# A decoder trunk's MLP: squared token factors at the additions to the residual, half of the first products in 512 columns, and a new order of one block

## The chip, the core and the metric

The kernel runs on one core of a Trainium2 chip. A core has five engines that run their own instruction streams and wait for each other by semaphores: TensorE (PE, matmuls into PSUM; its weight loads are shown as PEld), VectorE (DVE), ScalarE (ACT), GpSimd (POOL) and SyncE (SP, here a queue of DMA issues). The metric is the device time of one execution in microseconds, the median of several runs; lower is better.

## The reference, cut to what matters

Two layers over x, 256 tokens by 2048 columns, in float32: a recurrent block and an attention block, each followed by an MLP, and a last RMS norm. The MLP is what the change touches:

```python
def _rmsnorm(x, g):
    y = x32 * lax.rsqrt(jnp.mean(x32 * x32, axis=-1, keepdims=True) + EPS)
    return y * g

def _mlp(h, w1, w2):                       # w1 2048 x 8192, w2 8192 x 2048
    u = jnp.einsum('bsd,df->bsf', h, w1)
    u = jnp.square(jax.nn.relu(u))
    return jnp.einsum('bsf,fd->bsd', u, w2)

x = x + _mlp(_rmsnorm(x, mlp_norm[i]), mlp_w1[i], mlp_w2[i])
```

The norm's factor of a token, rstd (the reciprocal root of its mean square), is positive. So relu(rstd * v)^2 is rstd^2 * relu(v)^2, and the factor can stand before the square or, squared, behind the second product.

## The kernel before

**Units and items.** A unit is a matrix of 128 x 2048 weights: 1 MB that SP's queue loads (`raw`, or a tile `q..`), that ScalarE copies to a rounded part (`whi`, line 134) and VectorE subtracts to a remainder (`wlo`, line 138). Each product x * w is made of three matmul passes with these parts, x high * w high, x low * w high and x high * w low. Items are the steps of the program, mostly one unit each, in an order written out by hand. Around the item of unit i the code issues the load of unit i+5, ScalarE's `whi` up to i+3 and VectorE's `wlo` up to i+2. There are three buffers each for `whi` and `wlo`, so the `whi` of unit i+3 waits until PE has done unit i. `after(n, ...)` puts work behind the item that comes n later; additions to x (`take`, `closed`) come first there. Every engine works through its instructions in program order.

**The MLP** runs in eight parts p of 1024 hidden columns. The first product of a part is eight "w" items (j = 0 to 7): 128 hidden rows each, with the weights standing and the tokens moving. `stand_w` makes for each of 16 slices of the inner dimension three matmuls of 256 columns: `whi` with the tokens' high parts, `whi` with their low parts, `wlo` with the high parts. `stand_both`, used before in the recurrent block's gates and in the attention, moves high and low parts in one matmul of 512 columns, and one of 256 for `wlo`; the two halves of the bank are summed later. `u_done` takes relu times the token's rstd from PSUM to `uu` (line 603, VectorE, with rstd spread over all partitions as `rstdB`), squares it and copies it to its high part `aT` (lines 604 and 606, ScalarE), and one item later VectorE makes the low part (line 612).

**The second product** of parts 0 to 6 uses a scheme with seven products in place of eight for two halves of the tokens, of the hidden rows and of the output columns ("groups" 0 and 1: output columns 0 to 1023 and 1024 to 2047). Its items are b11, b21, t1, t2, b22, t3 and t4, 12 matmuls of 512 columns each. Sums of weights are made by VectorE (line 693: `qT`, for b11 and b22) or by POOL's adding transfers (line 689: q12 += q22 for b22, q21 += qT for t4); sums of tokens by VectorE (lines 623 to 636: `sw`, `sT`). Results are added to x by `take` (line 697). PSUM has eight banks: four (`acc`) hold the sums B, T and C of group 0 and B of group 1 over all parts, and are added to x only at the end of part 6, `ENDS` items after their product; the others are added to x after each part. A block is the 22 items of a part:

```python
2: (
    "w", "b11 0", "t1 0", "w", "b21 0", "b22 0", "t2 0", "w", "t3 0", "w", "t4 0", "b11 1", "t1 1", "w",
    "b22 1", "t2 1", "w", "t3 1", "b21 1", "w", "w", "t4 1",
),
```

Its w's make the first products of the next part. Counted from 0, they stand at 0, 3, 7, 9, 13, 16, 19 and 20, with j = 0, 4, 1, 5, 2, 6, 3, 7. Below, w13 is the w at place 13, and so on. (In the change below, the sixth w stands at place 17; w17 is that one, w16 the one before.) In part 0 the places 2 and 3 are exchanged. The last part, 7, has plain products only.

Of the kernel before, what the change touches and what calls it, by code (L numbers as in the profile page):

```python
# [32 lines left out]
for _name, _n in (("mix0", 16), ("mix1", 16), ("mlp0", 16), ("mlp1", 16), ("lam", 20),  # L33
# [9 lines left out]
SCRATCH = 4096  # L43
LOOK_LOAD = 5

CONV = (0, 2)

BOTH = range(3, 9)

ROWS = 5  # L50

# [8 lines left out]

ORDER = {
    0: ("s", "w") * 8,
    2: (
        "w", "b11 0", "t1 0", "w", "b21 0", "b22 0", "t2 0", "w", "t3 0", "w", "t4 0", "b11 1", "t1 1", "w",
        "b22 1", "t2 1", "w", "t3 1", "b21 1", "w", "w", "t4 1",
    ),
}

SUMS = {"b22": [("q12", "q12", "q22", "dma"), ("qT", "qT", "q22", "dve")],
        "t4": [("q21", "q21", "qT", "dma")],  # L70
        "b11": [("qT", "b11", "q12", "dve")]}

HELD = {0: ("B", "T", "C"), 2: ("B",)}

ENDS = {"t1 0": 12, "b21 0": 12, "b22 0": 18, "b21 1": 3}


@with_exitstack
def trunk(ctx: ExitStack, tc: tile.TileContext, a: dict, out: bass.AP):
# [194 lines left out]
    def new_ssq():  # L274
        state["ssq"] = perm.tile([P, NT, NCH], F32, name="ssq", bufs=2)

    def rstd_cols():
        v = perm.tile([P, 4, NT], F32, name="rs", bufs=2)
        nc.vector.tensor_reduce(v[:, 0, :], state["ssq"], axis=AX.X, op=OP.add)
        nc.vector.tensor_scalar(v[:, 0, :], v[:, 0, :], 1.0 / D, EPS, op0=OP.mult, op1=OP.add)  # L280
        nc.scalar.activation(v[:, 1, :], v[:, 0, :], AF.Sqrt)
        nc.vector.reciprocal(v[:, 2, :], v[:, 1, :])
        nc.vector.tensor_mul(v[:, 3, :], v[:, 2, :], v[:, 2, :])
        nc.vector.tensor_mul(v[:, 3, :], v[:, 3, :], v[:, 0, :])
        nc.vector.tensor_scalar(v[:, 3, :], v[:, 3, :], -0.5, 1.5, op0=OP.mult, op1=OP.add)
        nc.vector.tensor_mul(v[:, 2, :], v[:, 2, :], v[:, 3, :])
        state["rstd"] = v[:, 2, :]

    def rstd_rows():
        state["kick"] = True  # L290
# [22 lines left out]
            mm(ps, hi[:, s], xl, False, False)  # L313
            mm(ps, lo[:, s], xh, False, last and j == len(ks) - 1)

    def stand_both(ps, u):

        hi, lo = split[u]
        state["kick"] = False
        for k in range(KD):  # L320
            x, s = xT(k), slice(k * 128, (k + 1) * 128)
            mm(ps, hi[:, s], x.rearrange("p (t u q) -> p u q t", t=2, u=2), k == 0, False)
            mm(ps[:, :S], lo[:, s], moving(x, 0), False, k == KD - 1)
# [43 lines left out]
        for t in range(NT):  # L367
            nc.vector.tensor_add(xc[n][:, t, :], xc[n][:, t, :], acc[t])

    def close_chunk(n, gname, rows):  # L370
        def closed(acc):
            if n == 0:
                new_ssq()
            add_x(n, acc)
            if n < NCH - 1:
                square_sum(n)
            after(1, transpose_chunk, n, gname)
            if n == NCH - 1:
                after(1, square_sum, n)
                after(1, rstd_cols)  # L380
                if rows:
                    after(4, rstd_rows)
        return closed
# [148 lines left out]
    def plan_rec():  # L532
        def proj(h, j, g):
            u = unit(a["w_in"][(KR if g else 0) + 2 * h + j] if len(units) >= FIRST else a["w_first"][len(units)])

            done = gb_done if g else xb_done
            if u < FIRST:
                first[u] = (done, h, j)
                return

            bank = []

            def begin():
# [24 lines left out]

        def oproj(n, kq):
            u = unit(a["w_out"][n * 5 + kq])  # L570
            out_item(("o", n), u, aT, range(4 * kq, 4 * kq + 4), kq == 0, kq == 4,
                     close_chunk(n, "mlp0", True))

        for h in range(NB):
            proj(h, 0, 0)
            proj(h, 1, 0)
            proj(h, 0, 1)
            proj(h, 1, 1)
            if h:
# [18 lines left out]
    def u_done(p, j, ps):  # L598
        h, k = divmod(j, 4)
        if h == 0:  # L600
            squares[p, k] = lru.tile([P, 2, S], F32, name="uu", bufs=4)
        uu = squares[p, k][:, h, :]
        nc.vector.scalar_tensor_tensor(uu, ps[:, :S], 0.0, state["rstdB"], op0=OP.max, op1=OP.mult)
        nc.scalar.activation(uu, uu, AF.Square)
        t = new_aT(8 * (p % 2) + j)
        nc.scalar.activation(t[:, 0:256], uu, AF.Copy)
        after(1, u_low, t, uu)
        if h == 1 and GROUPS[p]:
            after(1, waiting.append, (p, k))

    def u_low(t, uu):
        nc.vector.tensor_sub(t[:, 256:512], uu, t[:, 0:256].bitcast(F32))
# [36 lines left out]
    def plan_mlp(w1, w2, done):  # L649
        def plan_first(p, j):  # L650
            u = unit(w1[8 * p + j])

            def run():
                accs["u", p, j] = acc_tile() if p == 0 else psum.tile([P, 512], F32, name="g", bufs=2)
                stand_w(accs["u", p, j][:, :S], u, range(KD), 0, True, True)
                after(0, u_done, p, j, accs.pop(("u", p, j)))
            item(u, run, "w")

        def plan_start():
            us = [unit(w1[j]) for j in (0, 4)]  # L660
            for at, ks in enumerate((range(0, 12), range(12, 16))):
                for u, j in zip(us, (0, 4)):
                    def run(u=u, j=j, ks=ks, at=at):
                        if at == 0:
                            accs["u", 0, j] = acc_tile()
                        stand_w(accs["u", 0, j][:, :S], u, ks, ks[0], at == 0, at == 1)
                        if at == 1:
                            after(1 if j == 0 else 0, u_done, 0, j, accs.pop(("u", 0, j)))
                    item(u, run)

        def plan_plain(p, n, h, last_part):
            u = unit(w2[((p // 2) * 4 + n) * 4 + (p % 2) * 2 + h])
            out_item(("m", n), u, aT, range(8 * (p % 2) + 4 * h, 8 * (p % 2) + 4 * h + 4), h == 0, h == 1,
                     done(n) if last_part else (lambda acc, n=n: add_x(n, acc)))

        def plan_group(p, n0, last_group):

# [15 lines left out]
                nc.vector.tensor_add(q[to], q[a], q[b])  # L693

            def take(n, t, b, sign):
                x = xc[n0 + n][:, t, :]
                (nc.vector.tensor_add if sign > 0 else nc.vector.tensor_sub)(x, x, bank[b])
# [200 lines left out]
    def plan_att():  # L898
# [61 lines left out]
    def final_add(acc, cols, t, base, to):  # L960

        x = xc[LAST][:, t, cols]
        nc.vector.tensor_add(x, x, acc[:, cols])
        junk = perm.tile([P, 512], mybir.dt.bfloat16, name="junk")
        nc.vector.tensor_tensor_reduce(junk[:, cols], x, x, 0.25 / D, base, OP.mult, OP.add, to)

# [284 lines left out]
```

## Time and profile before

| | |
|---|---|
| median of 3 runs | 2011.72 us (2011.59 to 2011.74) |
| the profiled execution | 2011.96 us, of which the span of its profile 2010.2 us |
| TensorE busy | 2000.4 us, 13569 matmuls, granted clock 0.999 |
| VectorE busy | 1732.4 us |
| ScalarE busy | 1291.9 us |
| HBM read | 409.59 MB, 205 GB/s over the span |
| first MLP, parts 0 to 6 | about 367 to 956 us of the span; a block repeats after 79.5 us |
| second MLP | about 1372 to 2002 us |

Busy time of TensorE is a cover, not a rate: the matmuls are pipelined, and the profile models their ends. A better measure is how long a piece of the chain takes for its number of matmuls. A row of the timeline has start, length, engine, line, operation and tiles; in brackets the idle time before it and what ended it. A row of windows has the window, its length, and per engine the busy time with the number of instructions.

### The profile page before, as it was taken

The numbers are of one execution on the slowest core, as the hardware profiler recorded it, in microseconds if no ns is written. First come the engines' busy times: TensorE is split into PE (matmuls) and PEld (weight loads), VectorE is DVE, ScalarE is ACT, GpSimd is POOL, SyncE is SP. The second block draws the span as 40 slices with busy tenths as digits, with TensorE's granted clock in tenths as the row PEclk, the third lists the DMA queues.
The fourth block names the chain that finished last, engine by engine and source line by source line (L and its number), as shares of the span: only waits on it lengthen the run. The fifth ranks groups of instructions, "written<-read, shape, count | busy, mean of one in ns | idle before, by whom it ended". The sixth has DMA issues, their size and how long they took to land.

```text
span 2010.2 us, 32554 instructions
## 1 busy us (share of the span) xinstructions
PE 2000.4 (100%) x13569; PEld 1870.2 (93%) x13569; DVE 1732.4 (86%) x1917; ACT 1291.9 (64%) x1426; POOL 95.4 (5%) x83
## 2 busy tenths in 40 slices
PE   9999999999999999999999999999999999999998
PEld 9999988999999999999889999889999999999997
DVE  7999975799999999998658969857999999999986
ACT  7788875566666666666557657656666666666663
POOL 0111110000000000000000000000000000000001
PEclk9999999999999999999999999999999999999999
DMA  8555565678788788787555555456787887887874
GB/s 311 210 189 204 190 229 197 241 248 252 264 284 268 226 293 271 247 250 244 206 213 173 187 190 183 173 199 242 250 252 262 288 266 227 295 272 246 249 245 165
DMA packets 69059, 472.51 MB, mean 235 GB/s; under 512 B 7600, under 2 KB 7984, under 8 KB 13616
## 3 DMA queue, kind: packets, MB, share of 16 engines
q1 hardware_dynamic: 60560, 411.19, 54.7%
q0 software_dynamic: 8064, 58.72, 14.9%
q8 instruction: 106, 1.74, 0.3%
q10 hardware_dynamic: 288, 0.52, 0.1%
q14 instruction: 41, 0.34, 0.0%
HBM read 409.59 MB, written 2.10 MB: 205 GB/s over the span
## 4 chain that ended last, share of the span: by engine, by line
PE 96%; DVE 3%; ACT 0%; issue 0%; DMA 0%
PE acc L203 46%; PE g L203 32%; PE tr L203 18%; DVE wlo L138 1%; PE tr L244 1%; DVE c L439 0%; PE tr L866 0%; ACT whi L134 0%; DMA xT<-in_begin 0%; DVE c L435 0%; DVE sT L636 0%; DVE glo L138 0%; DVE qT L693 0%; DVE gw L470 0%; ACT xc L979 0%
## 5 line engine op out<-in xcount | busy, mean ns | idle before, releaser
L134 ACT ACTIVATE whi<-raw 128x2048 fp32r<-128x2048 f32 (+1 forms) x309 | 568.4, 1844 | 294.7 <-PE acc L203 163.2
L138 DVE TENSOR_TENSOR wlo<-raw,whi 128x2048 fp32r<-128x2048 f32 (+1 forms) x309 | 678.1, 2198 | 92.3 <-ACT whi L134 91.9
L203 PE MATMUL g<-xT,whi 128*128 128x256 f32 x3649 | 617.0, 275 | 0.0
L203 PEld LDWEIGHTS g<-xT,whi 128*128 128x128 f32 x3649 | 554.0, 192 | 0.0
L203 PE MATMUL g<-xT,wlo 128*128 128x256 f32 x1824 | 502.9, 276 | 0.2 <-DVE wlo L138 0.2
L203 PE MATMUL acc<-xT,whi 128*128 128x256 f32 (+1 forms) x2020 | 453.7, 313 | 0.1
L203 PE MATMUL acc<-xT,wlo 128*128 128x256 f32 x1360 | 373.1, 274 | 0.5 <-DVE wlo L138 0.4
L203 PEld LDWEIGHTS g<-xT,wlo 128*128 128x128 f32 x1824 | 350.1, 192 | 1.5 <-DVE wlo L138 0.3
L203 PEld LDWEIGHTS acc<-xT,whi 128*128 128x128 f32 x2020 | 333.2, 191 | 19.1 <-ACT whi L134 1.0
L203 PE MATMUL acc<-whi,aT 128*128 128x512 f32 (+1 forms) x1086 | 322.9, 374 | 0.0
L138 DVE TENSOR_TENSOR wlo<-q,whi 128x2048 fp32r<-128x2048 f32 x112 | 256.0, 2286 | 28.0 <-ACT whi L134 27.8
L134 ACT ACTIVATE whi<-q 128x2048 fp32r<-128x2048 f32 x112 | 214.3, 1914 | 79.1 <-PE g L203 52.2
L203 PEld LDWEIGHTS acc<-xT,wlo 128*128 128x128 f32 x1360 | 261.2, 192 | 1.2 <-DVE wlo L138 1.1
L203 PEld LDWEIGHTS acc<-whi,aT 128*128 128x128 f32 x1086 | 204.0, 189 | 27.6
L203 PE MATMUL tr<-whi,sT 128*128 128x512 f32 (+1 forms) x728 | 212.7, 364 | 0.0
L203 PE MATMUL acc<-wlo,aT 128*128 128x512 f32 (+1 forms) x536 | 200.9, 376 | 0.0
L134 ACT ACTIVATE whi<-qT 128x2048 fp32r<-128x2048 f32 x56 | 107.5, 1919 | 127.7 <-PE g L203 93.2
L203 PEld LDWEIGHTS tr<-whi,sT 128*128 128x128 f32 x728 | 137.6, 189 | 20.5
L203 PE MATMUL tr<-whi,aT 128*128 128x512 f32 (+1 forms) x462 | 140.3, 373 | 0.0
L138 DVE TENSOR_TENSOR wlo<-qT,whi 128x2048 fp32r<-128x2048 f32 x56 | 128.0, 2286 | 1.3 <-ACT whi L134 1.3
L203 PE MATMUL tr<-wlo,sT 128*128 128x512 f32 x336 | 127.3, 379 | 0.0
L203 PEld LDWEIGHTS acc<-wlo,aT 128*128 128x128 f32 x536 | 101.1, 189 | 13.4 <-DVE wlo L138 0.2
(173 smaller groups left out, 2166.6 us busy)
## 6 DMA issues: line engine op xcount, KB each, us to landing
raw<-in_w SPq DMA_DIRECT2D x172, 1024.0 KB, 7.0
q<-in_w SPq DMA_DIRECT2D x84, 1024.0 KB, 8.2
raw<-in_w_in SPq DMA_DIRECT2D x35, 1024.0 KB, 4.7
raw<-in_w_qk SPq DMA_DIRECT2D x32, 1024.0 KB, 4.8
q<-q POOLq DMA_DIRECT2D x28, 1024.0 KB, 12.4
q<-qT POOLq DMA_DIRECT2D x28, 1024.0 KB, 7.5
raw<-in_w_out SPq DMA_DIRECT2D x20, 1024.0 KB, 4.7
raw<-in_w_v SPq DMA_DIRECT2D x16, 1024.0 KB, 4.8
```

Of the source, the lines that this page charges most:

```text
L134: nc.scalar.activation(split[i][0][:, s], r, AF.Copy)
L138: nc.vector.tensor_sub(split[i][1][:, s], r, split[i][0][:, s].bitcast(F32))
L203: nc.tensor.matmul(o, l, r, start=start, stop=stop, skip_group_check=True)
L244: nc.tensor.transpose(tr[:, k, t * 128:(t + 1) * 128], xc[n][:, t, c:c + 128], ident)
```

## The change

There are four edits.

1. `u_done` no longer multiplies by rstd. The additions of the MLP's products to x (`take`, `add_mlp`, `final_add`) become one instruction with a factor per token, x = product * rstd^2 + x (or with the negative of it, where the sign is minus). The factors are two more columns of `rstd_cols`; `rstd_rows`, which spread rstd over the partitions with two transposes and a copy, is not called for the MLPs.
2. The w's with j = 1, 2, 3, 6 in part 0, and with j = 1, 2, 4, 7 in the others, use `stand_both`. Their two halves are brought together by ScalarE (a copy of the second half to `uu`) and VectorE (a custom instruction, TENSOR_ADD_SAT: sum of both, held between 0 and the largest float, which is the relu). The other w's have their relu on ScalarE, straight from PSUM. For the wide ones the square follows one item later.
3. In group 1, b21 stands ahead of b22 and no longer behind t3.
4. The held banks are added to x 18 (T), 15 (B of group 0), 17 (C) and 4 items (B of group 1) after their product; before 12, 12, 18 and 3.

```diff
 ORDER = {
     0: ("s", "w") * 8,
-    2: (
-        "w", "b11 0", "t1 0", "w", "b21 0", "b22 0", "t2 0", "w", "t3 0", "w", "t4 0", "b11 1", "t1 1", "w",
-        "b22 1", "t2 1", "w", "t3 1", "b21 1", "w", "w", "t4 1",
-    ),
+    2: ("w", "b11 0", "t1 0", "w", "b21 0", "b22 0", "t2 0", "w", "t3 0", "w", "t4 0", "b11 1", "t1 1", "w", "b21 1", "b22 1", "t2 1", "w", "t3 1", "w", "w", "t4 1",),
 }
...
+WIDE = ((1, 2, 3, 6), (1, 2, 4, 7))
...
-ENDS = {"t1 0": 12, "b21 0": 12, "b22 0": 18, "b21 1": 3}
+ENDS = {'t1 0': 18, 'b21 0': 15, 'b22 0': 17, 'b21 1': 4}
...
+        if squared:
+            nc.vector.tensor_mul(v[:, 4, :], v[:, 2, :], v[:, 2, :])
+            nc.vector.tensor_scalar(v[:, 5, :], v[:, 4, :], -1.0, None, op0=OP.mult)
+            state["rstd2"] = v[:, 4:6, :]
...
+    def add_scaled(x, acc, t, sign=1):
+
+        i = 0 if sign > 0 else 1
+        nc.vector.scalar_tensor_tensor(x, acc, state["rstd2"][:, i, t:t + 1], x, op0=OP.mult, op1=OP.add)
+
+    def add_mlp(n, acc):
+        for t in range(NT):
+            add_scaled(xc[n][:, t, :], acc[t], t)
...
-                after(1, rstd_cols)
+                after(1, rstd_cols, not rows)
                 if rows:
                     after(4, rstd_rows)
...
-        nc.vector.scalar_tensor_tensor(uu, ps[:, :S], 0.0, state["rstdB"], op0=OP.max, op1=OP.mult)
+        if j in WIDE[p > 0]:
+            nc.scalar.activation(uu, ps[:, S:], AF.Copy)
+            after(0, u_sum, p, j, ps, uu)
+        else:
+            after(0, u_plain, p, j, ps, uu)
+
+    def u_plain(p, j, ps, uu):
+        nc.scalar.activation(uu, ps[:, :S], AF.Relu)
+        u_square(p, j, uu)
+
+    def u_sum(p, j, ps, uu):
+        nc.vector._custom_dve(TENSOR_ADD_SAT, out=uu, in0=ps[:, :S], in1=uu, s0=LARGEST, s1=0.0)
+        after(1, u_square, p, j, uu)
+
+    def u_square(p, j, uu):
+        h, k = divmod(j, 4)
         nc.scalar.activation(uu, uu, AF.Square)
         t = new_aT(8 * (p % 2) + j)
         nc.scalar.activation(t[:, 0:256], uu, AF.Copy)
         after(1, u_low, t, uu)
...
-                stand_w(accs["u", p, j][:, :S], u, range(KD), 0, True, True)
-                after(0, u_done, p, j, accs.pop(("u", p, j)))
+                first_product(accs["u", p, j], u, j, p)
+                u_done(p, j, accs.pop(("u", p, j)))
...
+        def first_product(ps, u, j, p, ks=range(KD)):
+            if j in WIDE[p > 0]:
+                stand_both(ps, u, ks)
+            else:
+                stand_w(ps[:, :S], u, ks, ks[0], ks[0] == 0, ks[-1] == KD - 1)
...
             def take(n, t, b, sign):
-                x = xc[n0 + n][:, t, :]
-                (nc.vector.tensor_add if sign > 0 else nc.vector.tensor_sub)(x, x, bank[b])
+                add_scaled(xc[n0 + n][:, t, :], bank[b], t, sign)
```

How the order changes shows at two places. The first is behind w13 of a block. On TensorE (`g` is the w's bank, `tr` and `acc` those of products) there stands before, where w13 ends and b22 1 begins:

```order
L203 MATMUL g<-xT_3869,whi 128x256 x2
L203 MATMUL g<-xT_3869,wlo 128x256
L203 MATMUL tr<-whi,sT_4038 128x512
L203 MATMUL tr<-wlo,sT_4038 128x512
L203 MATMUL tr<-whi,sT_4038 128x512
```

and in the change, where w13 is a wide one and b21 1 (the tokens' `aT`, in a held bank) begins:

```order
L204 MATMUL g<-xT_3869,whi 128x512
L204 MATMUL g<-xT_3869,wlo 128x256
L204 MATMUL acc<-whi,aT_4444 128x512
L204 MATMUL acc<-wlo,aT_4444 128x512
L204 MATMUL acc<-whi,aT_4444 128x512
```

Two matmuls of 256 columns have become one of 512, and b22 1 comes one product later. On VectorE there stands before at this place, from the `wlo` of w13 to that of w16 (the additions are line 697):

```order
L138 TENSOR_TENSOR wlo<-raw,whi 128x2048
L693 TENSOR_TENSOR qT<-qT,q_5506 128x2048
L697 TENSOR_TENSOR xc_70<-xc_70,tr 128x512
L138 TENSOR_TENSOR wlo<-q_5506,whi 128x2048
L697 TENSOR_TENSOR xc_71<-xc_71,tr 128x512
L138 TENSOR_TENSOR wlo<-qT,whi 128x2048
L603 SCALAR_TENSOR_TENSOR uu<-g,rstdB 128x256
L138 TENSOR_TENSOR wlo<-raw,whi 128x2048
```

and in the change, from the `wlo` of w13 to that of t2 1 (`q_5294` is b21 1's weights, `q_5372` b22 1's; line 630 is the custom sum, 378 the addition with a factor):

```order
L139 TENSOR_TENSOR wlo<-raw,whi 128x2048
L378 SCALAR_TENSOR_TENSOR xc_70<-tr,rs,xc_70 128x512
L139 TENSOR_TENSOR wlo<-q_5294,whi 128x2048
L733 TENSOR_TENSOR qT<-qT,q_5372 128x2048
L378 SCALAR_TENSOR_TENSOR xc_71<-tr,rs,xc_71 128x512
L139 TENSOR_TENSOR wlo<-q_5372,whi 128x2048
L630 ISA uu<-g,uu 128x256
L139 TENSOR_TENSOR wlo<-qT,whi 128x2048
```

The `wlo` of b21 1 has come in ahead of the sum of weights, and the addition of t1 1's bank (the second of the two; b22 1 writes to that bank next) now has w13 and b21 1 between its product and b22 1, before w13 alone. The second place is the end of the block, on VectorE. Before, from the `wlo` of the next block's first w (its j = 0) to the token sum behind the `wlo` of its b11:

```order
L138 TENSOR_TENSOR wlo<-raw,whi 128x2048
L693 TENSOR_TENSOR qT<-raw,q_5784 128x2048
L612 TENSOR_TENSOR aT_5842<-uu,aT_5842 128x256
L603 SCALAR_TENSOR_TENSOR uu<-g,rstdB 128x256
L138 TENSOR_TENSOR wlo<-raw,whi 128x2048
L697 TENSOR_TENSOR xc_70<-xc_70,tr 128x512
L612 TENSOR_TENSOR aT_5905<-uu,aT_5905 128x256
L623 TENSOR_TENSOR sw<-uu 128x2x128
```

and in the change:

```order
L139 TENSOR_TENSOR wlo<-raw,whi 128x2048
L733 TENSOR_TENSOR qT<-raw,q_5608 128x2048
L646 TENSOR_TENSOR aT_5666<-uu,aT_5666 128x256
L630 ISA uu<-g,uu 128x256
L670 TENSOR_TENSOR sT_5673<-sw,sT_5673 128x512
L139 TENSOR_TENSOR wlo<-raw,whi 128x2048
L378 SCALAR_TENSOR_TENSOR xc_70<-tr,rs,xc_70 128x512
L657 TENSOR_TENSOR sw<-uu 128x2x128
```

Here w20 has the custom sum in place of line 603, the low part of the third token sum stands one item later, and the low part of w20's `aT` has left this piece (it stands behind the next block's first w).

More of the change, by code (lines that the diff above doesn't have):

```diff
@@ L9 @@
 from concourse._compat import with_exitstack
+from concourse.dve_ops import TENSOR_ADD_SAT
 F32 = mybir.dt.float32
@@ L25 @@
 EPS = 1e-6
+LARGEST = float(np.finfo(np.float32).max)
 KD = D // 128
@@ L44 @@
 LOOK_LOAD = 5
+BOTH = range(3, 9)
 CONV = (0, 2)
-BOTH = range(3, 9)
 ROWS = 5
@@ L62 @@
     0: ("s", "w") * 8,
-    2: (
-        "w", "b11 0", "t1 0", "w", "b21 0", "b22 0", "t2 0", "w", "t3 0", "w", "t4 0", "b11 1", "t1 1", "w",
-        "b22 1", "t2 1", "w", "t3 1", "b21 1", "w", "w", "t4 1",
-    ),
+    2: ("w", "b11 0", "t1 0", "w", "b21 0", "b22 0", "t2 0", "w", "t3 0", "w", "t4 0", "b11 1", "t1 1", "w", "b21 1", "b22 1", "t2 1", "w", "t3 1", "w", "w", "t4 1",),
 }
-SUMS = {"b22": [("q12", "q12", "q22", "dma"), ("qT", "qT", "q22", "dve")],
+SUMS = {"b22": [("q12", "q12", "q22", "dma"), ("qT", "qT", "q22", ('dve', 'dve'))],
         "t4": [("q21", "q21", "qT", "dma")],
         "b11": [("qT", "b11", "q12", "dve")]}
+WIDE = ((1, 2, 3, 6), (1, 2, 4, 7))
 HELD = {0: ("B", "T", "C"), 2: ("B",)}
-ENDS = {"t1 0": 12, "b21 0": 12, "b22 0": 18, "b21 1": 3}
+ENDS = {'t1 0': 18, 'b21 0': 15, 'b22 0': 17, 'b21 1': 4}
 @with_exitstack
@@ L275, in new_ssq, with rstd_cols @@
         state["ssq"] = perm.tile([P, NT, NCH], F32, name="ssq", bufs=2)
-    def rstd_cols():
-        v = perm.tile([P, 4, NT], F32, name="rs", bufs=2)
+    def rstd_cols(squared=False):
+        v = perm.tile([P, 6, NT], F32, name="rs", bufs=2)
         nc.vector.tensor_reduce(v[:, 0, :], state["ssq"], axis=AX.X, op=OP.add)
@@ L314, in stand_w, with stand_both @@
             mm(ps, lo[:, s], xh, False, last and j == len(ks) - 1)
-    def stand_both(ps, u):
+    def stand_both(ps, u, ks=range(KD)):
         hi, lo = split[u]
         state["kick"] = False
-        for k in range(KD):
+        for k in ks:
             x, s = xT(k), slice(k * 128, (k + 1) * 128)
@@ L368, in add_x, with close_chunk @@
             nc.vector.tensor_add(xc[n][:, t, :], xc[n][:, t, :], acc[t])
-    def close_chunk(n, gname, rows):
+    def add_scaled(x, acc, t, sign=1):
[4 more added lines that the diff above has]
+            add_scaled(xc[n][:, t, :], acc[t], t)
+    def close_chunk(n, gname, add):
+        rows = add is add_mlp
         def closed(acc):
@@ L373, in closed @@
                 new_ssq()
-            add_x(n, acc)
+            add(n, acc)
             if n < NCH - 1:
@@ L571, in oproj @@
             out_item(("o", n), u, aT, range(4 * kq, 4 * kq + 4), kq == 0, kq == 4,
-                     close_chunk(n, "mlp0", True))
+                     close_chunk(n, "mlp0", add_x))
         for h in range(NB):
@@ L608, in u_done @@
         if h == 1 and GROUPS[p]:
-            after(1, waiting.append, (p, k))
+            if j in WIDE[p > 0]:
+                waiting.append((p, k))
+            else:
+                after(1, waiting.append, (p, k))
     def u_low(t, uu):
@@ L654, in run @@
                 accs["u", p, j] = acc_tile() if p == 0 else psum.tile([P, 512], F32, name="g", bufs=2)
-                stand_w(accs["u", p, j][:, :S], u, range(KD), 0, True, True)
-                after(0, u_done, p, j, accs.pop(("u", p, j)))
+                first_product(accs["u", p, j], u, j, p)
+                u_done(p, j, accs.pop(("u", p, j)))
             item(u, run, "w")
+        def first_product(ps, u, j, p, ks=range(KD)):
+            if j in WIDE[p > 0]:
+                stand_both(ps, u, ks)
+            else:
+                stand_w(ps[:, :S], u, ks, ks[0], ks[0] == 0, ks[-1] == KD - 1)
         def plan_start():
@@ L665, in run @@
                             accs["u", 0, j] = acc_tile()
-                        stand_w(accs["u", 0, j][:, :S], u, ks, ks[0], at == 0, at == 1)
+                        first_product(accs["u", 0, j], u, j, 0, ks)
                         if at == 1:
-                            after(1 if j == 0 else 0, u_done, 0, j, accs.pop(("u", 0, j)))
+                            u_done(0, j, accs.pop(("u", 0, j)))
                     item(u, run)
@@ L673, in plan_plain @@
             out_item(("m", n), u, aT, range(8 * (p % 2) + 4 * h, 8 * (p % 2) + 4 * h + 4), h == 0, h == 1,
-                     done(n) if last_part else (lambda acc, n=n: add_x(n, acc)))
+                     done(n) if last_part else (lambda acc, n=n: add_mlp(n, acc)))
         def plan_group(p, n0, last_group):
@@ L704, in make_all @@
                 def make_all():
-                    for m in SUMS.get(name, []):
-                        add(*m)
+                    for *m, by in SUMS.get(name, []):
+                        add(*m, by if isinstance(by, str) else by[n0 // 2])
                 u = form(load_all, make_all, lambda: q[source])
@@ L925, in oproj @@
             u = unit(a["w_o"][n * 4 + kq])
-            out_item(("a", n), u, aT, range(4 * kq, 4 * kq + 4), kq == 0, kq == 3, close_chunk(n, "mlp1", True))
+            out_item(("a", n), u, aT, range(4 * kq, 4 * kq + 4), kq == 0, kq == 3, close_chunk(n, "mlp1", add_x))
         for n in (0, 1):
@@ L941, in done @@
                 new_ssq()
-            add_x(n, acc)
+            add_mlp(n, acc)
             square_sum(n)
@@ L962, in final_add @@
         x = xc[LAST][:, t, cols]
-        nc.vector.tensor_add(x, x, acc[:, cols])
+        add_scaled(x, acc[:, cols], t)
         junk = perm.tile([P, 512], mybir.dt.bfloat16, name="junk")
@@ L1046, in trunk @@
     item(None, lambda: lru.open("mlp"))
-    plan_mlp(a["w1_0"], a["w2_0"], lambda n: close_chunk(n, "mix1", True))
+    plan_mlp(a["w1_0"], a["w2_0"], lambda n: close_chunk(n, "mix1", add_mlp))
     item(None, lru.close)
```

## The prediction

> **What bounds the kernel now.** I read the page first (busy times and the chain's shares), then TensorE's own waits, then the chain in order of time, and last the queue of VectorE (DVE) at the two places where the chain's pieces are longer than their matmuls need.
>
> ```profile
> PE 2000.4 (100%) x13569; PEld 1870.2 (93%) x13569; DVE 1732.4 (86%) x1917; ACT 1291.9 (64%) x1426; POOL 95.4 (5%) x83
> PE 96%; DVE 3%; ACT 0%; issue 0%; DMA 0%
> ```
> ```profile
> PE g L203 <- DVE junk L1067: 1.3, 1, 1.3
> PE acc L203 <- DVE wlo L138: 0.4, 1, 0.4
> PE g L203 <- DVE wlo L138: 0.2, 1, 0.2
> ```
> TensorE (PE) is busy for 2000.4 of 2010.2 us and its named waits sum to 1.9 us. So time comes only from PE's own stream: fewer or cheaper matmuls, or the short delays that the modelled ends cover. Those show in the chain (start, length, engine and number of matmuls):
>
> ```profile
> 449.11 5.34 PE tr L203 x25
> ...
> 488.85 5.54 PE g L203 x48
> 494.40 5.18 PE acc L203 x24
> 502.17 5.36 PE g L203 x48
> ...
> 515.49 7.78 PE tr L203 x37
> 523.27 5.36 PE g L203 x48
> 528.63 5.33 PE tr L203 x25
> 533.96 5.36 PE g L203 x48
> 544.51 10.72 PE g L203 x96
> 557.83 5.36 PE g L203 x48
> 568.38 5.54 PE g L203 x48
> ...
> 1069.05 10.48 PE acc L203 x64
> ...
> 1891.76 5.54 PE g L203 x48
> ...
> 1931.53 5.33 PE tr L203 x25
> ```
> One first-product unit ("w") is 48 matmuls of 256 columns in 5.36 us: 111.7 ns each. The attention's q and k units do the same columns as 16 matmuls of 512 and 16 of 256: two units take 10.48, so 5.24 each. Three products of 12 matmuls take 7.78, 2.59 each; but the pair b22 1 and t2 1 behind w takes 5.33 to 5.34, 0.15 too long, in each of the 14 blocks with products (first and last shown). And the second w of a block takes 5.54, 0.18 too long, in 12 blocks.
>
> **The change part by part.** *512 columns.* Four of eight w's in each of 16 part-steps, 64 units, lose 16 matmuls each: 64 x (5.36 - 5.24) = **7.7 us** gained, all on PE. Nearest rows bound it: nothing (the columns are the same) and 7.7; I take 7.7, since the attention's units come from the same helper with operands laid out alike; a loss is excluded while a 512-column matmul takes 215.8 ns (494.40) and two of 256 take 223.4. The Trainium skill ("TensorE: Matmul & The Clock Gate", Back-to-back issue gap) puts a matmul at N/2.4 + 2.5 ns. By that two of 256 cost 2.5 ns more than one of 512, which is 2.6 us for the 1024 pairs. The trace agrees for 512 columns (494.40: 5.18 us for 24, 215.8 ns each) but has 111.7, not 109.2, for 256, and its whole units decide.
>
> *b21 1 ahead of b22 1.* What the pair waits for is on DVE:
>
> ```profile
> 525.51 2.29 DVE L138 TENSOR_TENSOR wlo<-q,whi 128x2048 fp32r<-128x2048 f32 x1
> 527.71 0.68 DVE L697 TENSOR_TENSOR xc<-xc,tr 128x512 f32<-128x512 f32 x1
> ```
> b22 1 adds to the bank that t1 1 has filled; the addition of that bank to x ends at 528.39 and PE is there at 528.63 less the lead of a weight load. With b21 1 (a held bank, nothing to wait for) in between, PE comes 2.6 us later: 14 x 0.15 = **2.1 us** gained; bounds 0 and 2.1. What is late next there: three products follow w, so DVE must give three wlo's in 7.8 us. DVE's instructions follow each other 0.08 us before the one ahead ends (558.92 + 2.28 = 561.20 against 561.12, rows below): wlo and a sum of weights take 2.20 of its queue, uu or the low part of aT 0.34, an addition 0.60, in the new form 0.67. DVE has idle time behind w7 (PE's end 507.53), so I walk from there. ScalarE's Copy and whi (0.39 + 1.92) let the wlo of t4 0 start at 509.85. To the end of b22 1's wlo stand six wlo's, two sums, four additions and two low parts: 13.2 + 4.4 + 2.7 + 0.7 = 21.0, that is 530.9. PE comes to b22 1 after t3 0, w9, three products, w13 and b21 1: 507.53 + 2.59 + 5.36 + 7.78 + 5.24 + 2.59 = 531.1, and wants wlo one matmul (0.2) later: 0.4 us to spare. For t2 1 DVE adds a custom sum and a wlo (2.6), PE a product (2.59): again 0.4. Covered, thinly; each 0.1 us beyond that costs 1.4 us over the 14 blocks.
>
> *The second w of a block.* DVE is in one unbroken run up to it:
>
> ```profile
> 541.19 2.29 DVE L138 TENSOR_TENSOR wlo<-raw,whi 128x2048 fp32r<-128x2048 f32 x1 [1.41 <-ACT whi L134]
> ...
> 552.91 0.42 DVE L603 SCALAR_TENSOR_TENSOR uu<-g,rstdB 128x256 f32<-128x256 f32 x1
> ...
> 558.25 0.42 DVE L612 TENSOR_TENSOR aT<-uu,aT 128x256 fp32r<-128x256 f32 x1
> 558.58 0.42 DVE L603 SCALAR_TENSOR_TENSOR uu<-g,rstdB 128x256 f32<-128x256 f32 x1
> 558.92 2.28 DVE L138 TENSOR_TENSOR wlo<-raw,whi 128x2048 fp32r<-128x2048 f32 x1
> 561.12 0.68 DVE L697 TENSOR_TENSOR xc<-xc,tr 128x512 f32<-128x512 f32 x1
> ...
> 565.24 0.42 DVE L603 SCALAR_TENSOR_TENSOR uu<-g,rstdB 128x256 f32<-128x256 f32 x1
> 566.18 2.28 DVE L138 TENSOR_TENSOR wlo<-raw,whi 128x2048 fp32r<-128x2048 f32 x1
> ```
> ```profile
> 541.19:568.46 27.27, 26.99 (x33) 1.00 0.97 321
> ```
> The run starts 1.87 us after PE's end of the w ahead (533.96 + 5.36 = 539.32: ACT's whi) and ends at 568.46, 29.14 after it; PE is at the second w 29.06 after it (568.38). In the change the run starts with the wlo of w20, one item later (its whi waits for the end of w17, as now that of w19 for w16). It holds one wlo less (558.92 to 561.12: 2.20), two uu less (0.34 each: w19 and w22 keep 256 columns and take ScalarE's Relu), and two additions to x that cost more:
>
> ```profile
> L697 DVE TENSOR_TENSOR xc<-xc,tr x140: 678/680/683, 408.4 to 1962.8; 128x512 f32<-128x512 f32 x140
> L788 DVE SCALAR_TENSOR_TENSOR av<-acc,rs,av x8: 741/746/751, 1039.7 to 1185.8; 128x512 fp32r<-128x512 f32 x8
> L965 DVE CUSTOM_DVE_ANT_0 junk<-xc,fs x3: 485/485/752, 1997.7 to 2002.8; 128x256 bf16<-128x256 f32 x2, 128x512 bf16<-128x512 f32 x1
> ```
> An addition with a factor per token is of L788's form: 0.07 more. The sum of the halves (w20) is a custom instruction: between uu's 0.42 and L965's 0.49. So the run is 27.27 - 2.20 - 0.68 + 0.14 = 24.53, or 24.60. PE's way loses b21 1 (2.59) and 0.12 for w20: 29.06 - 2.71 = 26.35. The run ends 1.87 + 24.53 = 26.40 to 26.47 after the start: 0.05 to 0.12 behind PE, against 0.08 now. So this wait stays: 0.15 to 0.22 for 0.18. I put down **0.3 us** lost in 12 blocks (0.02 each); bounds: gone (2.2 gained) and 0.1 worse (1.2 lost).
>
> *Factors at the additions.* rstd's rows are no longer spread for the two MLPs: 4 transposes leave PE.
>
> ```profile
> 366.48 0.22 PE tr L293 x2
> ```
> 2 x 0.22 = **0.4 us** gained. Two small instructions more in the column of factors lie ahead of the first addition by a whole block. The 128 uu leave DVE, 64 custom sums come; ScalarE gets 64 Relu and 64 Copy of 0.39 us:
>
> ```profile
> L792 ACT ACTIVATE y<-acc 128x256 f32<-128x256 f32 x32 | 12.3, 386 | 0.7
> ```
> That is 8 x 0.39 = 3.1 us in a block of 79.5 (568.38 less 488.85), on an engine at 64%. It is not on the path where ScalarE's whi ends DVE's idle time (541.19): the w ahead of it keeps 256 columns, so no Copy stands before that whi. If that cover went, 0.39 x 12 = 4.7 us. The last addition of the kernel, behind the last matmul, costs 0.06 more: **0.1 lost**. The held banks' new places (18, 15, 17 and 4 items after their product) only move ten additions (five per MLP) within the last block with products, in which DVE makes no token sums: nothing; if all stood in PE's way, 10 x 0.75 = 7.5 us, or as much gained if they stand in it now.
>
> **Sum**: 7.7 + 2.1 + 0.4 - 0.3 - 0.1 = 9.8 us. The profiled execution took 2011.96 (span 2010.2): 2002.2, span 2000.4. The runs' median is 0.24 lower: **2001.9**.
>
> **The rivals.** *The second w's wait goes* (DVE gains more than I count): 2.2 and the 0.3 more, **1999.4**. For it: DVE loses 64 instructions. Against: the run starts with ScalarE's whi, not with DVE's backlog, so earlier savings don't enter it.
>
> *512 columns give less.* If only a third of the 7.6 ns per pair came from the split, and the rest from the alternation of whi and wlo weights, which stays, 5.1 of the 7.7 us would be missing: **2007.0**. Against it: the units at 1069.05 alternate just so and take 5.24. The rule of the Trainium skill's page named above would leave just such a third.
>
> *DVE or ScalarE late at the second w.* The Square of w20 now stands one item later, behind the whi of t1, and the token sums on DVE wait for it; that whi waits for DVE's sum for b11, so the Square is done some 2.4 us (1.92 and itself) behind it, while DVE has a low part, the custom sum, a low part of 512 columns, wlo and an addition to make first (0.34 + 0.34 + 0.60 + 2.20 + 0.67 = 4.1): 1.7 us to spare. If other waits ate that and 0.6 us more: 12 x 0.6 = 7.2 lost, **2009.1**, no change.
>
> *A transfer takes the place of the wait: slower.* b21 1's load now stands on SP's queue ahead of t2 1's, and waits for the buffer that t4 0 frees:
>
> ```profile
> 504.94 0.42 SPq L685 DMA_DIRECT2D q<-in_w  x1
> ...
> 511.73 0.33 SPq L685 DMA_DIRECT2D q<-in_w  x1
> ```
> ```profile
> DMA to landing us min/median/max: 4.6/8.2/12.1
> ```
> ```profile
> DMA to landing us min/median/max: 6.9/9.7/13.8
> ```
> (first the loads of q, then POOL's adding transfers; then ScalarE's whi)
> ```profile
> L134 ACT ACTIVATE whi<-q 128x2048 fp32r<-128x2048 f32 x112 | 214.3, 1914 | 79.1 <-PE g L203 52.2 <-PE tr L203 13.7 <-DMA q<-qT 10.4
> ```
> So q22 is asked for at 512.1 instead of 504.94; it must land, be added to q12 by POOL's transfer, and pass whi and wlo (1.91 + 2.29) before t3 1, where PE comes at 531.1 + 2 x 2.59 + 5.36 = 541.6. Medians: 512.1 + 8.2 + 9.7 + 4.2 = 534.2; both maxima: 542.2, 0.6 late. Only with both transfers beyond that does it decide: from 1 us late the gain is gone in 14 blocks plus the bound of 4 us. At 2 us late: 28 - 9.8 = 18 lost, **2030**.
>
> **How the numbers follow.** About 0.2% (4 us) is what a measurement of this kernel can tell from no change. Chances: my sum with its bounds (2000.5 to 2004.5) 0.66; wait gone 0.12; 512 columns give less 0.06; late at the second w 0.11; transfer 0.05. Faster by over 0.2% (below 2007.7) takes the first two, most of the third and a third of the fourth: 0.86; same 0.09; slower 0.05. The range leaves out the transfer and the worse half of the late case, and reaches below to the wait gone with 0.6 to spare: 1998.8 to 2007.0.
>
> **What would show it.** In the profile after: w's of 32 matmuls in 5.24 us (512 columns); b22 1 and t2 1 in 5.18 beside b21 1, with no 5.33 (the order); the second w of a block 0.15 to 0.22 over its 5.24 (the wait that stays); four transposes of rstd instead of eight, and some 1030 matmuls fewer; ScalarE busy some 50 us more (128 x 0.39) and DVE some 14 less (64 x 0.42 less, 167 additions x 0.07 more). I am wrong if w's of 32 matmuls take 5.3 or more, if PE comes to t3 1 or t2 1 behind a gap, or if PE names waits for wlo of more than a few us.

## The result and the profile after

The changed kernel takes 2001.47 us (median of 6 runs, 2001.24 to 2002.05) against 2011.73 for the kernel before beside it (2011.42 to 2012.79): a ratio of 0.9947, 95% interval 0.9936 to 0.9957. 10.3 us are gained; 2001.9 was forecast. The profiled execution took 2001.35 us, its span 1999.6.

The page's line of busy times and the first line of its chain, after:

```profile
PE 1989.5 (99%) x12539; PEld 1832.1 (92%) x12539; DVE 1718.0 (86%) x1857; ACT 1323.0 (66%) x1552; POOL 95.1 (5%) x83
PE 97%; DVE 2%; ACT 0%; DMA 0%; issue 0%
```

TensorE still sets the end, with 1030 matmuls fewer, most of them the 64 x 16 of the wide units. The chain in order of time, after (start, length, engine, matmuls), for a block from its second w to the next block's:

```profile
487.26 5.40 PE g L204 x32
...
500.44 5.24 PE g L204 x32
...
513.63 7.83 PE tr L204 x37
...
529.29 5.18 PE tr L204 x25
534.48 5.36 PE g L204 x48
...
566.18 5.39 PE g L204 x32
```

A block takes 566.18 - 487.26 = 78.92 us, before 568.38 - 488.85 = 79.53. w7 (500.44) has 32 matmuls in 5.24, and so have w13 and w20. The pair b22 1 and t2 1 (529.29) takes 5.18 without the 0.15. The second w (487.26, 566.18), the block's fourth wide one, is still late, by 0.15 to 0.16 over 5.24. And one thing is new: t4 0, b11 1 and t1 1 (513.63) take 7.83 for 7.78. So 4 x 0.12 + 0.15 + 0.03 - 0.05 = 0.61 per block, the difference of the two block times.

### The profile page after: what moved, and what is told of

Same layout as the page of the kernel before. It is cut to its first block, busy times and chain, and to the rows that moved or that the text cites. A ratio compares the mean times of both kernels' runs of the same rounds, so it can differ in the third digit from the quotient of the medians.

```text
span 1999.6 us, 30557 instructions
## 1 busy us (share of the span) xinstructions
PE 1989.5 (99%) x12539; PEld 1832.1 (92%) x12539; DVE 1718.0 (86%) x1857; ACT 1323.0 (66%) x1552; POOL 95.1 (5%) x83
## 4 chain that ended last, share of the span: by engine, by line
PE 97%; DVE 2%; ACT 0%; DMA 0%; issue 0%
PE acc L204 46%; PE g L204 32%; PE tr L204 18%; DVE wlo L139 1%; PE tr L245 1%; DVE c L455 0%; PE tr L905 0%; DMA xT<-in_begin 0%; DVE c L451 0%; ACT whi L135 0%; DVE glo L139 0%; DVE gw L486 0%; ACT xc L1018 0%; DVE i L539 0%; DVE xb L444 0%
## 5 line engine op out<-in xcount | busy, mean ns | idle before, releaser
L204 PE MATMUL g<-xT,whi 128*128 128x256 f32 (+1 forms) x2753 | 610.5, 310 | 0.0
L204 PEld LDWEIGHTS g<-xT,whi 128*128 128x128 f32 x2753 | 451.5, 191 | 21.8
L204 PEld LDWEIGHTS acc<-xT,whi 128*128 128x128 f32 x1890 | 318.1, 191 | 22.7 <-ACT whi L135 1.1
L620 ACT ACTIVATE uu<-g 128x256 f32<-128x256 f32 x56 | 21.5, 383 | 156.2 <-PE g L204 156.2
```

The costliest lines, as they stand in the source:

```text
L204: nc.tensor.matmul(o, l, r, start=start, stop=stop, skip_group_check=True)
L620: nc.scalar.activation(uu, ps[:, S:], AF.Copy)
```

## Experiments

Each median is that of 5 to 11 executions. Each kernel is compared with executions of the kernel before that were made beside it, whose medians were 2011.73 (the change), 2012.12 (the four rows below it), 2012.27 (the next four) and 2012.23 us (the last two); expectations were written against 2011.7. Diffs are against the changed kernel unless said otherwise.

| kernel | median us | against before, us | ratio, 95% interval |
|---|---|---|---|
| the change | 2001.47 | -10.3 | 0.9936 to 0.9957 |
| narrow: no 512 columns | 2007.78 | -4.3 | 0.9969 to 0.9987 |
| order of before | 2005.82 | -6.3 | 0.9959 to 0.9982 |
| ends of before | 2003.15 | -9.0 | 0.9942 to 0.9970 |
| low part twice | 2007.88 | -4.2 | 0.9970 to 0.9988 |
| factors alone | 2011.79 | -0.5 | 0.9989 to 1.0007 |
| halves | 2000.59 | -11.7 | 0.9930 to 0.9955 |
| all wide | 2019.65 | +7.4 | 1.0025 to 1.0050 |
| halves, more wide | 2001.68 | -10.6 | 0.9937 to 0.9964 |
| the same, mended | 1996.94 | -15.3 | 0.9912 to 0.9936 |
| order alone | 2016.60 | +4.4 | 1.0012 to 1.0030 |

### What 512 columns are worth

```diff
-WIDE = ((1, 2, 3, 6), (1, 2, 4, 7))
+WIDE = ((), ())
```

> The changed kernel with all first products as 48 matmuls of 256 columns (edit 2 undone; factors, order and places of the held banks stay). My theory: each of the 64 units goes back from 5.24 to 5.36 us on TensorE, +7.7; VectorE's run before the second w of a block loses the custom sum of w20 (0.34) while TensorE's way grows by 0.12, so the wait of 0.15 there goes, -1.8: 2001.5 + 7.7 - 1.8 = 2007.4 us, w's all at 5.36, the second one too. Rival A, two matmuls of 256 columns cost only 2.5 ns more than one of 512: +2.6 and -1.8, 2002.3. Rival B, the wait is a fixed cost at that place: +7.7 alone, 2009.2 us.

Measured: 6.0 us less gain than the change (4.3 for 10.3); expected were 5.9. The chain in order of time of this kernel:

```profile
488.81 5.36 PE g L204 x48
...
515.27 7.81 PE tr L204 x37
...
568.04 5.36 PE g L204 x48
```

All w's take 5.36, and the second (488.81, 568.04) has no wait. A block takes 79.23, 0.31 more: 4 x 0.12 lost, 0.15 gained at the second w, 0.02 at t1 1. The split itself is worth the 7.7 us; by the rule of the Trainium skill that the prediction weighs ("TensorE: Matmul & The Clock Gate", Back-to-back issue gap), an estimate of 2.6 would be left of it, and the narrow units don't follow that rule (last section).

### The order, beside the rest and alone

```diff
-    2: (... "t1 1", "w", "b21 1", "b22 1", "t2 1", "w", "t3 1", "w", "w", "t4 1",),
+    2: (... "t1 1", "w", "b22 1", "t2 1", "w", "t3 1", "b21 1", "w", "w", "t4 1",),
-ENDS = {'t1 0': 18, 'b21 0': 15, 'b22 0': 17, 'b21 1': 4}
+ENDS = {'t1 0': 18, 'b21 0': 15, 'b22 0': 17, 'b21 1': 3}
```

> The changed kernel with the order of before in group 1 (b22 1 right behind w13, b21 1 behind t3 1, its bank added 3 items behind it); factors and 512 columns stay. My theory: the addition of t1 1's bank to x on VectorE ends after TensorE could begin b22 1, and costs the more since an addition takes 0.07 longer: wait of some 0.5 us at b22 1 in 14 blocks (+7), while the run before the second w has 2.6 us more of TensorE's way and 2.2 more of a wlo, so the wait of 0.15 there goes (-1.8): 2006.5 us (2003.6 to 2008). Rival, the edits add up as in the kernel before: only the 0.15 of the pair b22 1 and t2 1 comes back, 14 x 0.15 = 2.1: 2003.6 us.

Measured: 4.0 lost against the change, between the theory (5) and the rival (2.1). The chain, and TensorE's wait (total, times, longest), of the kernel with the order of before:

```profile
527.50 5.42 PE tr L207 x25
...
567.21 5.24 PE g L207 x32
...
646.40 5.24 PE g L207 x32
```
```profile
PE tr L207 <- DVE xc L381: 2.6, 14, 0.2
```

The wait at b22 1 is the named 0.18 and 0.24 in the pair's 5.42: 0.42 where I had worked out 0.5. The wait at the second w is gone. Its block takes 646.40 - 567.21 = 79.19, 0.27 more than after (0.42 - 0.15); 14 times that is 3.8. So the order is worth nearly twice the 0.15 per block that it removes: with the factors and the wide w13 the old order would have made that wait larger.

The new order alone, on the kernel before:

```diff
-    2: (... "w", "b22 1", "t2 1", "w", "t3 1", "b21 1", "w", "w", "t4 1",),
+    2: (... "w", "b21 1", "b22 1", "t2 1", "w", "t3 1", "w", "w", "t4 1",),
-ENDS = {"t1 0": 12, "b21 0": 12, "b22 0": 18, "b21 1": 3}
+ENDS = {"t1 0": 12, "b21 0": 12, "b22 0": 18, "b21 1": 4}
```

> The kernel before with the new order of group 1 alone (edit 3; b21 1's bank added 4 items behind it): rstd still taken at uu, first products of 256 columns. My theory: the pair b22 1 and t2 1 falls to 5.18 (14 x 0.15 = 2.1 gained), but VectorE's run ahead of the second w loses 2.20 where TensorE's way loses 2.59, so the wait there grows from 0.18 to 0.57 in 12 blocks, 4.7 lost: 2011.7 + 2.6 = 2014.3 us. Rival: the order's gain stands by itself, 2009.6.

It is slower than before, by 4.4 us. From its chain in order of time:

```profile
489.79 5.40 PE g L200 x46
...
532.02 5.18 PE tr L200 x25
...
569.55 5.40 PE g L200 x46
...
936.54 5.40 PE g L200 x46
```

The pair takes 5.18, as the rival has it too. But the chain now jumps to VectorE's `wlo` inside the second w: 46 matmuls are left behind the wait (489.79, 569.55), which is 0.53 with the matmul behind it, and the block takes 79.76 for 79.53. The theory had 0.57. It lacked the last block with products, where w17 waits in the same way (936.54, and again at 1944.41 in the second MLP; 0.55 each), and 0.8 at the second MLP's first block. 12 x 0.35 - 2.1 + 1.1 + 0.8 = 4.0 of the 4.4.

### The factors alone

```diff
-WIDE = ((1, 2, 3, 6), (1, 2, 4, 7))
+WIDE = ((), ())
...and the order and ENDS of the kernel before
```

> The kernel before with the squared factors alone (edit 1): first products of 256 columns, order and places of the held banks as before. My theory: VectorE loses its two uu in the run ahead of the second w, so the wait of 0.18 there goes (12 x 0.18 = 2.2), but the addition of t1 1's bank ends later against TensorE than before: the wait at b22 1 was 0.42 in the run with the order of before and 512 columns, where TensorE came 0.12 earlier, so 0.30 here for 0.15 (14 x 0.15 = 2.1 lost), and 0.03 at t1 1 (0.4 lost); 4 transposes less give 0.4. Together nothing: 2011.6 us where the kernel before takes 2011.7. Rival: the additions' 0.07 do not reach TensorE, the wait at b22 1 stays 0.15: 2.2 + 0.4 gained, 2009.1.

In this kernel every relu is ScalarE's. No difference can be measured (-0.5), as the theory says. Its chain in order of time shows the two effects that cancel:

```profile
489.08 5.36 PE g L207 x48
...
515.53 7.81 PE tr L207 x37
523.35 5.36 PE g L207 x48
528.77 5.42 PE tr L207 x25
...
568.61 5.36 PE g L207 x48
```

The second w has lost its 0.18, while the pair has gone from 5.33 to 5.42 and starts 0.06 behind the end of w13 (523.35 + 5.36 = 528.71), and t1 1 has gone from 7.78 to 7.81. So the wait at b22 1 is 0.24 + 0.06 = 0.30, as the theory has it, and 2.2 + 0.4 - 2.1 - 0.4 = 0.1 by these rows. The block takes 568.61 - 489.08 = 79.53, as before. Factors alone give -0.5, the order alone +4.4, and both with the new ends -4.3 (the narrow kernel): the factors pay by giving VectorE the time that the order takes away.

### The held banks' places

```diff
-ENDS = {'t1 0': 18, 'b21 0': 15, 'b22 0': 17, 'b21 1': 4}
+ENDS = {"t1 0": 12, "b21 0": 12, "b22 0": 18, "b21 1": 3}
```

> The changed kernel with the held banks added at the places of before (12, 12, 18 and 3 items behind their product). My theory: the ten additions lie in the last block with products, where VectorE makes no token sums and has time: no change, 2001.5 us within 0.5. Rival: some stand in TensorE's way at the old places, up to 10 x 0.75 = 7.5 more, 2009 us.

1.3 us are lost, not nothing. VectorE's queue in the last block with products, in this kernel, and its chain at that place:

```profile
926.41 1.41 DVE L378 SCALAR_TENSOR_TENSOR xc<-acc,rs,xc 128x512 f32<-128x512 f32 x2
927.73 2.28 DVE L139 TENSOR_TENSOR wlo<-raw,whi 128x2048 fp32r<-128x2048 f32 x1
```
```profile
930.07 5.40 PE g L204 x46
```

Two held banks (`acc`) are added between the `wlo` of t2 1 and that of w17, which then ends at 930.01; TensorE goes on with w17 at 930.07, 0.6 us late, once in each MLP (the second time at 1930.74). In the changed kernel w17 takes 5.36 there. The last block has no token sums, but the thin place is elsewhere: where three products follow w13. The kernel with the order alone has two held banks at the same place of the queue, and loses its 0.55 there; the kernel before, which has two products behind w13, has no such wait (931.82, 5.36 for 48 matmuls). So the new places make up for a loss that the new order brings.

### The run ahead of the second w

Twice the low part of w19's `aT`:

```diff
         after(1, u_low, t, uu)
+        if p and j == 3:
+            after(1, u_low, t, uu)
```

> The changed kernel with the low part of aT of w19 (j = 3) made twice by VectorE, 0.34 us more in its unbroken run ahead of the second w of each of 12 blocks (the same values are written again). My theory: that run, from ScalarE's whi behind w17 to the second w's wlo, sets the second w, so the wait of 0.15 becomes 0.49: +12 x 0.34 = 4.1, 2005.6 us. Rival: the 0.15 is a fixed cost of that place and the run has slack: 2001.5 us.

6.0 us are lost against the change. VectorE's queue in this kernel, and its chain:

```profile
558.10 0.88 DVE L648 TENSOR_TENSOR aT<-uu,aT 128x256 fp32r<-128x256 f32 x2
```
```profile
489.77 5.29 PE g L204 x31
...
569.15 5.29 PE g L204 x31
```

The block takes 79.38, 0.46 more than after. The second low part writes the same tile and starts only when the first is through: the two take 0.88, and the run has grown by 0.46 instead of 0.34. 12 x 0.46 = 5.5 of the 6.0. What VectorE does in this run goes to the end one to one; there is no slack.

The other way, the weights with which the run begins in two pieces:

```diff
+        if units[i].get("halves"):
+            raw[i] = [(slice(at, at + 1024), r[:, at:at + 1024]) for at in (0, 1024)]
+            nc.sync.dma_start(r, ap)
+            return
...
             u = unit(w1[8 * p + j])
+            units[u]["halves"] = p > 0 and j == 7
```

> The changed kernel, in which the weights of w20 (the ones with which VectorE's run ahead of the second w begins) are cut into whi and wlo in two pieces of 1024 columns each. VectorE can begin on the first piece when ScalarE has done half. My theory: the run starts some 0.85 us earlier behind w17, and the second w's wait of 0.15 goes in 12 blocks: 1.8 gained, 1999.7 us where the changed kernel takes 2001.5. Rival: the run is held by a later whi or by ScalarE's high part of a token sum, and ends where it did: 2001.5.

1.4 us more are gained than by the change (11.7 for 10.3). The start of the run on VectorE after the change, and in the kernel with halves, and that kernel's chain:

```profile
541.71 2.29 DVE L139 TENSOR_TENSOR wlo<-raw,whi 128x2048 fp32r<-128x2048 f32 x1 [1.98 <-ACT whi L135]
```
```profile
541.38 2.36 DVE L143 TENSOR_TENSOR wlo<-raw,whi 128x1024 fp32r<-128x1024 f32 x2 [1.12 <-ACT whi L139]
```
```profile
566.71 5.24 PE g L208 x32
```

VectorE's idle time ahead of the run falls from 1.98 to 1.12, for 0.07 more of its busy time, and the second w takes 5.24. The interval (0.9930 to 0.9955, 5 us wide) is wider than the 1.4; the rows decide.

### How far 512 columns go

```diff
-WIDE = ((1, 2, 3, 6), (1, 2, 4, 7))
+WIDE = (tuple(range(8)), tuple(range(8)))
```

> The changed kernel with all eight first products of every part in 512 columns. My theory: 64 more units at 5.24 for 5.36 give 7.7, but w17's Copy (0.28 of ScalarE's way) now stands ahead of the whi that starts VectorE's run, the run gets two custom sums more (0.34 each), and TensorE comes to the second w 0.24 earlier: 1.2 us more of wait there in 12 blocks, 14.4 lost. 2001.5 - 7.7 + 14.4 = 2008 us (2005 to 2011). Rival: what counts is TensorE's matmuls, VectorE has slack: 2001.5 - 7.7 = 1993.8.

7.4 us slower than before, where 3.7 faster was expected and 18 faster by the rival. The chain's second w, and TensorE's waits, of this kernel:

```profile
490.79 5.29 PE g L204 x31
...
570.96 5.29 PE g L204 x31
```
```profile
PE g L204 <- DVE wlo L139: 7.3, 12, 0.6
PE acc L204 <- DVE wlo L139: 6.9, 17, 1.3
PE tr L204 <- DVE xc L378: 3.7, 14, 0.3
```

A block takes 80.17, 1.25 more than after although its matmuls need 0.48 less. Before the second w and in the product ahead of it TensorE loses 1.43 (the expected wait was 1.35). What I had left out is the third row: t1 1 is late by 0.5 in all 14 blocks, 7 us, since w9 is a wide one too; and some 1.5 in the first block of each MLP.

```diff
-WIDE = ((1, 2, 3, 6), (1, 2, 4, 7))
+WIDE = ((1, 2, 3, 6), (0, 1, 2, 4, 5, 7))
...with the weights of w20 and of t4 0 in halves
```

> The changed kernel with the weights of w20 and of t4 0 (those that start VectorE's two runs of a block) cut in halves, and with w0 and w9 (j = 0 and 5) of parts 1 to 7 in 512 columns as well. My theory: the halves give each run some 0.85 us; w0 costs the first run 0.34 + 0.12, w9 the second 0.34, so both waits (0.15 at the second w, 0.05 at t1 1) go: 1.8 + 0.7 gained, and 28 units x 0.12 = 3.4: 2001.5 - 5.9 = 1995.6 us. Rival: the halves give nothing, the two sums come on top of the waits: 12 x 0.46 + 14 x 0.34 = 10.3 lost against 3.4, 2008.4 us.

Between theory and rival: about what the change gives. Its chain, VectorE's queue and ScalarE's at t1 1, and TensorE's wait as the trace names it:

```profile
520.85 2.83 PE tr L210 x13
...
568.28 5.24 PE g L210 x32
```
```profile
517.75 2.29 DVE L145 TENSOR_TENSOR wlo<-qT,whi 128x2048 fp32r<-128x2048 f32 x1 [0.60 <-ACT whi L141]
519.96 0.75 DVE L384 SCALAR_TENSOR_TENSOR xc<-tr,rs,xc 128x512 f32<-128x512 f32 x1
```
```profile
515.53 0.38 ACT L626 ACTIVATE uu<-g 128x256 f32<-128x256 f32 x1 [2.57 <-PE g L210]
515.81 1.90 ACT L141 ACTIVATE whi<-qT 128x2048 fp32r<-128x2048 f32 x1
```
```profile
PE tr L210 <- ACT aT L643: 2.4, 14, 0.2
```

The second w is good (5.24), but t1 1 is 0.41 late. VectorE was idle for 0.60 ahead of the `wlo`: it waited for `whi`, which w9's Copy (line 626) has pushed back by 0.28. So the wait can be a chain from w9's end: Copy, whi, wlo, and the addition that frees the bank. The addition ends at 520.71, t1 1 begins at 520.85. The trace names another releaser, ScalarE's high part of an `aT`, so this kernel alone does not decide it; the next one does. The wait is there although the weights of t4 0 are cut in halves. The same chain without the Copy makes the 0.05 of the changed kernel. Its VectorE and ScalarE:

```profile
515.54 2.28 DVE L139 TENSOR_TENSOR wlo<-qT,whi 128x2048 fp32r<-128x2048 f32 x1
517.74 0.74 DVE L378 SCALAR_TENSOR_TENSOR xc<-tr,rs,xc 128x512 f32<-128x512 f32 x1
```
```profile
513.56 1.92 ACT L135 ACTIVATE whi<-qT 128x2048 fp32r<-128x2048 f32 x1 [2.58 <-PE g L204]
```

w9 ends at 513.63 by the chain, the whi at 515.48, the addition at 518.48, and TensorE wants t1 1 at 513.63 + 2 x 2.59 = 518.81 less the lead of a weight load. The addition's 0.07 more is about the size of the wait.

The mended version, its diff against the kernel just shown:

```diff
-                units[u]["halves"] = name == "t4" and n0 == 0
+                units[u]["halves"] = (name, n0) in (("t4", 0), ("t1", 2))
...
-WIDE = ((1, 2, 3, 6), (0, 1, 2, 4, 5, 7))
+WIDE = ((1, 2, 3, 6), (1, 2, 4, 5, 7)) + ((0, 1, 2, 4, 5, 7),) * 6
...and WIDE[p] where WIDE[p > 0] stood
```

> The run with halves and more wide units, mended at its two losses: w0 made in block 0 of each MLP stays at 256 columns (it cost 1.4 us there in the first MLP), and the weights of t1 1 are cut in halves too. My theory: the wait at t1 1 is a chain, from TensorE's end of w9 over whi (1.92) and wlo (2.28) of t1 1's weights to the addition (0.75) behind them that frees its bank; with halves the wlo starts some 0.7 us earlier and the wait of 0.41 goes in 14 blocks. Then all gains stand: second w 1.8, t1 1 0.7, 26 units x 0.12 = 3.1: 2001.5 - 5.6 = 1995.9 us. Rival: the wait at t1 1 comes from ScalarE's high part of aT, as the trace names it, and stays at 0.41 (14 x 0.36 more than in the changed kernel): 2001.5 - 1.8 - 3.1 + 5.0 = 2001.6.

15.3 us less than the kernel before, 5.0 less than the change; expected were 5.6, and the rival would have given nothing. It is the fastest of all kernels here. Its chain, and VectorE's queue and ScalarE's high part at t1 1:

```profile
387.49 8.17 DMA q<-in_w
...
417.49 2.64 PE acc L210 x11
...
514.28 7.78 PE tr L210 x37
...
566.66 5.24 PE g L210 x32
```
```profile
515.85 2.35 DVE L145 TENSOR_TENSOR wlo<-qT,whi 128x1024 fp32r<-128x1024 f32 x2
```
```profile
519.16 0.42 ACT L643 ACTIVATE aT<-uu 128x256 fp32r<-128x256 f32 x1
```

Both waits are gone. So the wait at t1 1 was the chain over whi, wlo and the addition, not ScalarE's high part of aT, which the trace names: here that high part ends at 519.58, and t1 1 has begun at 519.30, ahead of it. What is missing of the 5.6 lies in the first block of the first MLP, which is 0.85 slower than that of the second: there the chain enters b22 0 behind VectorE (417.49). It goes back to a load of q asked for at 387.49, which took 8.17 us; the same load took 6.9 after the change. It took 8.3 in the kernel shown just before, whose 1.4 us at that place I had put down to w0. So keeping w0 narrow has not taken this loss away, and what makes the load longer is open.

## Why the prediction was right, point by point

- **512 columns, 7.7.** Right: 5.24 and 5.36 in the rows, and 6.0 net by the narrow kernel.
- **b21 1 ahead of b22 1, 2.1.** Right as a change of the pair (5.18), and the walk through VectorE's queue held. It put b22 1's wlo at 530.9 with w7's end at 507.53, 23.4 after it; now w7 ends at 505.68 and that wlo 23.26 later, at 528.94:

```profile
526.66 2.28 DVE L139 TENSOR_TENSOR wlo<-q,whi 128x2048 fp32r<-128x2048 f32 x1
```

  TensorE wants it at 529.29 + 0.2: 0.55 to spare for the 0.4 worked out. As the worth of the edit, 2.1 was too small: 4.0 without it.
- **The second w, 0.3 lost.** The place, the mechanism and the run's length held. The run's last wlo ends at 566.22, so the run takes 566.22 - 541.71 = 24.51 against 24.53:

```profile
563.94 2.28 DVE L139 TENSOR_TENSOR wlo<-raw,whi 128x2048 fp32r<-128x2048 f32 x1
```

  The wait is 0.15 to 0.16, the lower end of 0.15 to 0.22, so the term is 0.4 gained instead of 0.3 lost. The rival that it goes fell; it needed the halves. The rival of a late ScalarE fell by the margin worked out for it: the Square of w20 ends at 558.09 and VectorE's token sum starts at 559.82, 1.7 us to spare.
- **Factors.** Four transposes are gone (0.4). ScalarE is busy 31 us more where I had 50 (1323.0 less 1291.9); Copy takes 0.38 and Relu 0.36, and each overlaps a neighbour in ScalarE's queue by some 0.1, which the 0.39 from a row of its own does not show. VectorE lost 14.4 for "some 14"; the figures given there (64 x 0.42 less 167 x 0.07) make 15.2. The step that failed is small: of "an addition costs 0.07 more" I followed two places and not the third, t1 1, where TensorE now waits 0.05 in 14 blocks, 0.7 us lost (0.03 of the 0.05 is there with the factors alone).
- **Held banks, nothing.** Mis-sized: kept at their old places they would cost 1.3. The bounds (7.5 both ways) held.
- **The transfer.** q22 was asked for at 510.67 and landed at 518.94; the adding transfer took from 519.50 to 532.37, 12.9 us for the median of 9.7 that I took. ScalarE waited for it, and TensorE did not:

```profile
532.45 1.92 ACT L135 ACTIVATE whi<-q 128x2048 fp32r<-128x2048 f32 x1 [0.39 <-DMA q<-q]
```

  Its wlo ends at 536.87 and t3 1 begins at 534.48 + 5.36 = 539.84: 3 us to spare.

The sum by these rows is 7.7 + 2.1 + 0.4 + 0.4 - 0.7 - 0.1 = 9.8, the forecast's 9.8 with two errors of 0.7 that cancel: that the sum came out so close is luck. The median fell by 10.3, the span by 10.6. In the two profiled executions the stretches of the two MLPs fell by 10.3 together (359.66 to 955.68 and 1364.96 to 1960.72 before, 359.46 to 950.19 and 1359.48 to 1950.20 after), where the terms above, without the last addition, give 9.9. Of the 0.4 between them, 0.2 is a wait that one block before had beside its steady ones: the second w's at 647.90 and 807.17, two blocks apart, are 159.27 apart for 2 x 79.53. What made the rest, no run tells.

## What to carry to other kernels

Where one engine sets the end and another runs behind it without slack, count the second engine's run between two fixed points (what starts it, what it must deliver) and the first engine's way between the same points: the difference is the wait, and each edit moves both. Edits that are worth nothing or less alone can pay together, since one brings the time that the other spends. Where such a run starts with a copy on a third engine, cut the copy in two, so that the run begins on the first half.

## What the runs showed of the hardware

Part of what a wide unit gains lies in the matmuls that were not changed. In a narrow unit all matmuls start 111.7 ns apart. In a wide one, those of 512 columns and of 256 take turns, here in TensorE's timeline after:

```profile
502.13 0.27 PE L204 MATMUL g<-xT,wlo 128*128 128x256 f32 x1
502.24 0.38 PE L204 MATMUL g<-xT,whi 128*128 128x512 f32 x1
502.46 0.27 PE L204 MATMUL g<-xT,wlo 128*128 128x256 f32 x1
```

Over this unit the next matmul comes 218.5 ns after the start of one of 512 columns and 109.0 after that of one of 256: 327.5 for 335. So of the 7.5 ns per pair, 2.7 come from the 256-column matmul behind the wide one, and 4.9 from the one wide matmul in place of two (218.5 for 223.4). The Trainium skill ("TensorE: Matmul & The Clock Gate", Back-to-back issue gap) gives 109.2 ns for 256 columns by its formula for the gap of single matmuls at the full clock: the trace agrees where they stand between wide ones (109.0), and has 111.7 where only 256-column matmuls follow each other. The wide ones between them are in turn followed after 218.5, and not after the 215.8 of a stream of 512-column matmuls (494.40 before: 5.18 us for 24). What makes these 2.5 to 2.7 ns, no run tells.
